# A hybrid decoder step on one core: pools that wait tile by tile, and a 4 MB write moved from the head of the SyncE queue to its tail

## The chip, the core and the metric

The kernel runs on one NeuronCore of a Trainium2 chip. The core has a matrix engine (TensorE, "PE" in the profile, with weight loads "PEld"), a vector engine (DVE), a scalar engine (ACT), GpSimd (POOL) and SyncE (SP), which here only issues transfers. Each engine works through its own instructions in order and waits on semaphores. Transfers are carried by 16 DMA engines; those issued by SP go through one queue (q1, "hardware_dynamic"), those issued by POOL through another (q0, "software_dynamic"). The metric is the device time of one execution in microseconds (us), the median of the runs shown.

## The reference

The program is one inference step of a two-layer decoder: 1024 new prompt tokens with 16 meta tokens ahead of them, and 8 running sequences with one new token each ("the samples"). Layer 0 mixes with gated linear attention, layer 1 with differential attention; each is followed by a squared-ReLU MLP, and every residual goes through a layer norm. All values are 32-bit floats. Cut to what matters:

```python
for layer in range(DEPTH):                       # 2
    if layer % 2 == 0:
        f_p, st_p = gla_prompt(x_p, ...)         # 1024 + 16 tokens, chunked recurrence
        f_s, st_s = gla_sample(x_s, state_gla, ...)   # 8 sequences with a 4 MB state
    else:
        f_p, k_p, v_p = diff_prompt(x_p, ...)    # causal attention, 8 heads, two softmaxes
        f_s, k_s, v_s = diff_sample(x_s, cache_k, cache_v, page_table, ...)  # 4096 past rows in pages
    x_p = post_norm(x_p, f_p, ln_mix_g[layer], ln_mix_b[layer])
    x_s = post_norm(x_s, f_s, ln_mix_g[layer], ln_mix_b[layer])
    x_p = post_norm(x_p, sq_relu_mlp(x_p, mlp_w1[layer], mlp_w2[layer]), ln_mlp_g[layer], ln_mlp_b[layer])
    x_s = post_norm(x_s, sq_relu_mlp(x_s, mlp_w1[layer], mlp_w2[layer]), ln_mlp_g[layer], ln_mlp_b[layer])
y_prompt = x_p[:, N_META:]

def post_norm(x, f, g, b):                       # (z - mean) * rsqrt(var + eps) * g + b
    return layer_norm(DEEPNORM_ALPHA * x + f, g, b)
```

The last line of the last norm adds `ln_mlp_b[1]`, one row of 1024 values, to each of the 1024 rows of `y_prompt`.

## The kernel before

**How products are made.** Most products split each 32-bit operand into a high and a low part of a shorter format and sum three matmuls (`mm3`, lines 185 to 188: L186 high x high, L187, L188 the cross terms). For weights, ACT rounds the loaded tile (`raw` or `rw`) to `whi` and POOL subtracts to get `wlo` (L173, L174; in the last MLP L1386, L1387). The samples' products are plain 32-bit matmuls of narrow operands (L271, L276, L440, L494, L511 in the first stage, L1405 in the last).

**The stages.** (1) Prompt rows are loaded and transposed; the GLA layer runs head by head (q, k, v, decay levels, state updates). Among its matmuls stands the whole chain of the samples through layer 0 and up to layer 1's projections: sample weights come through two 1 MB buffers (`swt`, L214 and L220), the products are L271 and L276, the state of each sequence is loaded (L401), used (L404), updated and written back (L408). (2) Output projection and MLP of layer 0, with the key pages of the samples (L728 reads a page number from the table `ptab` on SP, L730 loads the page) multiplied on DVE and POOL beside it. (3) Projections of layer 1 and the value pages (L802). (4) Causal attention head by head, from L1074 on: a mask tile `cmask` and two tiles `vm` are cleared first, scores go through DVE (L1154) into `as`. (5) Output projection and the MLP of layer 1, written as a seven-product scheme: for each of 4 groups of hidden units seven "up" products, then seven "down" products. `operands` loads and splits what one product needs, while the product before it is half done (`mlp1`: `if t == 2: nxt = operands(...)`). `weight_operand` loads four 256 KB tiles of a weight (L1383) on SP; where a term is a difference of two weights a second load adds onto it from POOL (L1385); in some of the down products (in group 3 in the second and third) it also loads the raw rows of w2 for the samples (L1390, tiles `rw`, five buffers) and calls `beside`, the matmul L1405 into the samples' sums. `chip_operand` reads split activations that an earlier group has kept in DRAM (`XH<-xc`, POOL's queue, L1349).

**The end.** `last` scales each finished row tile and adds it into `y_prompt` in DRAM by an accumulating transfer from POOL (L1305, L1311). So `y_prompt` must hold the norm's offset by then: L1505 writes `ln_mlp_b[1]`, broadcast to 1024 rows, 4 MB from DRAM to DRAM on SP's queue. In the source it stands behind the last up product of group 3 (`if g == 3 and up and i == 7`).

**What sets the order.** A planner with a cost model orders each engine's instructions: what is ready sooner goes sooner, ties go by place in the source. L1505 depends on nothing, and the planner puts it near the head of SP's queue. `tc.issue_after(x)` lets the instructions traced in its block stand behind instruction x on the same engine; it sets the order of issue and adds no wait for x to end.

**Pools.** Tiles live in pools. A pool opened over the bytes of a closed one must wait for the users of these bytes. In the kernel before, the first use of such a pool waits for all the users of the closed pools beneath it. The pools of the stages: `gp` to `s2p` in stage 1, then `kp`, `dp`, `dp2`, `pgp` for the decode, `hp`/`ht`, `rp`/`qt`/`ht`, `a1` to `scp` for attention, and `hp`, `ht`, `rwp` for the last MLP.

Of the kernel before, what the change touches and what calls it, by code (L numbers as in the profile page):

```python
# [18 lines left out]
PSUM = bass.MemoryType.PSUM  # L19
# [3 lines left out]
D = 1024  # L23
T = 1024
# [11 lines left out]
PGB = 8  # L36
HOLD = (6, 8)
HTB = 1
# [72 lines left out]
def hybrid_step(ctx, tc, A, dbg=None, upto=9):  # L111
    nc = tc.nc
    V, S, G, TE = nc.vector, nc.scalar, nc.gpsimd, nc.tensor
    dma = nc.sync.dma_start
# [1 line left out]
    def bc(ap, shape, axis):  # L116
        return ap.unsqueeze(axis).broadcast_to(shape)

    cp = ctx.enter_context(tc.tile_pool(name="cp", bufs=1))
    wsp = ctx.enter_context(tc.tile_pool(name="wsp", bufs=2))  # L120
    wrp = ctx.enter_context(tc.tile_pool(name="wrp", bufs=2))
    mm = ctx.enter_context(tc.tile_pool(name="mm", bufs=3, space=PSUM))
    ax = ctx.enter_context(tc.tile_pool(name="ax", bufs=3, space=PSUM))
    sm = ctx.enter_context(tc.tile_pool(name="sm", bufs=2, space=PSUM))

    def mmt():
        return mm.tile([P, 512], F32, name="mmt")
# [1 line left out]
    def axt():  # L129
        return ax.tile([P, 512], F32, name="axt")  # L130
# [58 lines left out]


    p1 = ExitStack()
    gp = p1.enter_context(tc.tile_pool(name="gp", bufs=1))
    g2 = p1.enter_context(tc.tile_pool(name="g2", bufs=2))
    g8 = p1.enter_context(tc.tile_pool(name="g8", bufs=5))
    swp = p1.enter_context(tc.tile_pool(name="swp", bufs=2))
    spool = p1.enter_context(tc.tile_pool(name="spool", bufs=1))
    s2p = p1.enter_context(tc.tile_pool(name="s2p", bufs=2))

    def t2():
        return g8.tile([P, 512], F32, name="t2")  # L200
# [10 lines left out]
    def sload(src):  # L211

        t = swt()
        dma(t.rearrange("p k n -> p (k n)"), src)  # L214
        return t.rearrange("p k n -> p (k n)")
# [292 lines left out]
    for k in range(NB):  # L508
        t = sload(wd[k * P : (k + 1) * P, 0:2048])
# [48 lines left out]
    for h in range(GH):  # L558
# [3 lines left out]
        for c in range(2):  # L562
            cs = slice(512 * c, 512 * c + 512)
            for i in range(2):
# [3 lines left out]
                t = g2.tile([P, 512], F32, name=("gq", "gk")[i])  # L568
# [20 lines left out]
        for c in range(2):  # L589
# [58 lines left out]
            for i in range(4):  # L648
# [8 lines left out]
                t = 4 * c + i  # L657
# [33 lines left out]
        return dbg(locals())  # L691


    kp = ctx.enter_context(tc.tile_pool(name="kp", bufs=1))
    de = ExitStack()
    dp = de.enter_context(tc.tile_pool(name="dp", bufs=1))
    dp2 = de.enter_context(tc.tile_pool(name="dp2", bufs=2))
    pgp = de.enter_context(tc.tile_pool(name="pgp", bufs=PGB))
    bg_at = [10 ** 7]

    @contextmanager
# [230 lines left out]
    def alpha_row(v, op):  # L932

        for j in range(4):
            hs = slice(256 * j, 256 * j + 256)
            r = ht.tile([P, 256], F32, name="ht")
            dma(r, v[:, hs].broadcast_to([P, 256]))
            for t in (0, 4):
                y = Yt[:, t : t + 4, hs]
                rb = bc(r, [P, 4, 256], 1)  # L940
                if op == ALU.mult:
                    steps_v.append(V.scalar_tensor_tensor(y, y, ALPHA, rb, ALU.mult, ALU.mult).ins)
                else:
                    V.scalar_tensor_tensor(y, rb, ALPHA, y, ALU.mult, ALU.add)
            yield j
# [47 lines left out]


    e = ExitStack()
    hp = e.enter_context(tc.tile_pool(name="hp", bufs=1))
    ht = e.enter_context(tc.tile_pool(name="ht", bufs=HTB))
    HH = hp.tile([P, 4, T], F32R, name="HH")
    HL = hp.tile([P, 4, T], F32R, name="HL")
    for u in range(4):  # L1000
# [8 lines left out]


    e = ExitStack()
    rp = e.enter_context(tc.tile_pool(name="rp", bufs=1))
    qt = e.enter_context(tc.tile_pool(name="qt", bufs=3))
    ht = e.enter_context(tc.tile_pool(name="qht", bufs=2))
# [50 lines left out]

    de.close()
    e = ExitStack()
    a1 = e.enter_context(tc.tile_pool(name="a1", bufs=1))
    a2 = e.enter_context(tc.tile_pool(name="a2", bufs=4))
    a3 = e.enter_context(tc.tile_pool(name="a3", bufs=6))  # L1070
    scp = e.enter_context(tc.tile_pool(name="scp", bufs=5))
    CW = 448
    cm = a1.tile([P, CW], F32, name="cmask")
    V.memset(cm[:, : CW - P], 0.0)  # L1074
# [150 lines left out]


    e = ExitStack()
    hp = e.enter_context(tc.tile_pool(name="hp", bufs=1))
    ht = e.enter_context(tc.tile_pool(name="ht", bufs=HTB))
    rwp = e.enter_context(tc.tile_pool(name="rwp", bufs=5))  # L1230
# [23 lines left out]
    def rawt():  # L1254
        return rwp.tile([P, 512], F32, name="rw")
# [80 lines left out]
            dma(A["y_sample"][:, 0, u * 512 : (u + 1) * 512], sev[NM : NM + NS, :])  # L1336

    count = [0, 0]

    def chip_operand(terms, quarter, n, tmp, kept=None):  # L1340


        buf = XH.t[count[0] % 2].rearrange("p k n -> p (k n)")
        count[0] += 1
        parts = [buf[:, i * 4 * TH : i * 4 * TH + 4 * n] for i in range(2)]
        hi, lo = (x.rearrange("p (k n) -> p k n", n=n) for x in parts)
        if kept and kept[1]:
            for i in range(2):
                nc.gpsimd.dma_start(parts[i], kept[0][:, i])  # L1349
# [12 lines left out]
        if kept:  # L1362
            for i in range(2):
                nc.gpsimd.dma_start(kept[0][:, i], parts[i])
        return hi, lo

    def weight_operand(terms, quarter, side=None, beside=None):

        hi, lo = (wsp.tile([P, 2048], F32R, name=n).rearrange("p (k n) -> p k n", n=512) for n in ("whi", "wlo"))
        run = terms[0] == "run"  # L1370

        def src(q, k):
            w, r0, c0 = quarter(*q)
            return w[r0 + k * P : r0 + (k + 1) * P, c0 : c0 + 512]

        for k in range(4):
            if run or (len(terms) > 1 and terms[-1] != "new"):
                t = RW[:, k, :]
            else:
                count[1] += 1  # L1380
                t = wrp.tile([P, 512], F32, name="raw") if count[1] % 7 in (0, 3) else rawt()
            if not run:
                dma(t, src(terms[0], k))  # L1383
            if len(terms) > 1:
                nc.gpsimd.dma_start(t, src(terms[1], k), accum_op=ALU.add)  # L1385
            S.copy(hi[:, k, :], t)  # L1386
            G.tensor_tensor(lo[:, k, :], t, hi[:, k, :].bitcast(F32), op=ALU.subtract)  # L1387
            for q in side or ():
                t = rawt()
                dma(t, src(q, k))  # L1390
                beside(k, t, *q)
        return hi, lo
# [78 lines left out]
    def mlp1():  # L1471
        seq = []
        for g in range(4):
            seq += [(g, 1, i) for i in (1, 2, 5, 6, 4, 3, 7)]
            seq += [(g, 0, i) for i in ((1, 5, 6, 3, 7, 4, 2) if g < 3 else (1, 5, 6, 7, 4, 3, 2))]
        nxt = operands(*seq[0])
        n = 0
        for at, (g, up, i) in enumerate(seq):
            now = nxt
            if not up and i == 1:  # L1480
                if g == 0:
                    with tc.issue_after(steps_v[-1]):
                        list(alpha_row(A["ln_mix_g"][1:2], ALU.mult))
                    beta = alpha_row(A["ln_mix_b"][1:2], ALU.add)
                else:
                    for _ in range(2):
                        next(beta, None)
            for t in range(4):
                if t == 2 and at + 1 < len(seq):
                    nxt = operands(*seq[at + 1])  # L1490
                if up:
                    for c in range(2):
                        n += 1
                        up_tile(g, i, t, c, *now, axt() if n % 2 else mmt())
                    continue
                n += 1
                down_tile(g, i, t, *now, axt() if n % 2 else mmt())
                if g == 3:
                    for c, u in {7: [(1, 1)], 4: [(1, 0)], 3: [(0, 1)], 2: [(0, 0)]}.get(i, ()):
                        yield 4 * c + t, u  # L1500
            if g == 3 and not up and i == 6:
                samples_out()
            if g == 3 and up and i == 7:
                dma(fg, A["ln_mlp_g"][1:2].broadcast_to([P, D]))
                dma(A["y_prompt"][0], A["ln_mlp_b"][1:2].broadcast_to([T, D]))  # L1505
# [32 lines left out]
```

## Time and profile before

| | |
|---|---|
| median of 3 runs | 2943.17 us (2936.04 to 2952.23) |
| profiled execution | 2949.14 us, its span 2946.3 us |
| granted TensorE clock, mean | 0.977 |
| TensorE busy | 2789.4 us (95%) |
| DMA | 647.48 MB, mean 220 GB/s |
| SP's queue / POOL's queue, share of 16 engines | 53.3% / 16.0% |
| length of the write L1505 | 4096 KB |

A row of the timeline gives start, duration, engine, line, operation, tiles and count; in brackets stands the idle time before it and what ended it. `SPq` rows are issues of transfers by SP, so their duration is that of the issue. A 32-bit sample matmul shows as two records, so that a group of four has x8. A row of waits gives who waited for whom, the total in us, how often, and the longest.

### The profile page before, as it was taken

The page shows a single profiled execution, that of the slowest core. Times are in us where ns is not written, and L with a number is a line of the kernel's source. Part 1 is how long each engine was busy: PE and PEld are TensorE (multiplying, and loading weights), DVE is VectorE, ACT ScalarE, POOL GpSimd, SP SyncE. Part 2 cuts the span into 40 slices and gives each one's busy share as a digit, 9 for nine tenths or more (in the row PEclk, how much of TensorE's full clock was granted, in tenths as well). Part 3 has the DMA queues.
Part 4 walks back from the last instruction along what each step waited for, and adds up shares of the span by engine and source line. Part 5 has one row for each costly group of instructions (what it writes and reads, how often), then busy time and mean ns, then how long its engine had stood idle before and what let it go on. Part 6 is the DMA issues. An engine that isn't in the chain of part 4 may idle for free. (4 is left out here: it accounts for less than half of the span.)

```text
span 2946.3 us, 52168 instructions
## 1 busy us (share of the span) xinstructions
PE 2789.4 (95%) x19668; PEld 2274.8 (77%) x19668; DVE 1858.8 (63%) x2972; ACT 1038.9 (35%) x2072; POOL 1123.3 (38%) x871
## 2 busy tenths in 40 slices
PE   7899989999999999999999998989998999999996
PEld 4666667997777777777898896878888889797875
DVE  2464552546977777777757851778637755738278
ACT  2333433242221221131331111667524635345343
POOL 1231212224433333343233331023235766666665
PEclk9999999999999999999999999899999999999998
DMA  9565761513698988989477999355337878796883
GB/s 261 175 214 202 255 209 36 200 51 116 225 341 295 325 309 317 341 302 324 170 246 245 330 350 342 78 118 116 114 104 203 226 226 235 198 282 158 265 212 72
DMA packets 300203, 647.48 MB, mean 220 GB/s; under 512 B 35168, under 2 KB 150880, under 8 KB 288688
## 3 DMA queue, kind: packets, MB, share of 16 engines
q1 hardware_dynamic: 266976, 530.62, 53.3%
q0 software_dynamic: 32976, 113.55, 16.0%
q8 instruction: 154, 2.52, 0.4%
q14 instruction: 97, 0.79, 0.1%
HBM read 586.56 MB, written 45.11 MB: 214 GB/s over the span
## 5 line engine op out<-in xcount | busy, mean ns | idle before, releaser
L174 POOL TENSOR_TENSOR wlo<-raw,whi 128x512 fp32r<-128x512 f32 x256 | 359.6, 1417 | 748.6 <-ACT whi L173 671.2
L186 PE MATMUL mmt<-whi,XH 128*128 128x256 f32 (+1 forms) x1760 | 526.1, 301 | 4.7 <-DVE qr L1042 2.0
L187 PE MATMUL mmt<-wlo,XH 128*128 128x256 f32 (+1 forms) x1760 | 524.9, 299 | 0.9 <-POOL wlo L174 0.9
L186 PE MATMUL mmt<-XH,whi 128*128 128x512 f32 (+1 forms) x1216 | 438.4, 361 | 9.5 <-DVE HL L183 6.7
L188 PE MATMUL mmt<-XH,wlo 128*128 128x512 f32 (+1 forms) x1216 | 436.7, 360 | 0.0
L188 PE MATMUL mmt<-whi,XL 128*128 128x256 f32 x1536 | 434.1, 284 | 1.8 <-DVE XL L183 1.8
L762 DVE TENSOR_REDUCE sc<-pg 128x16 f32<-128x1024 f32 x256 | 309.6, 1214 | 103.0 <-POOL pg L761 99.7
L173 ACT CAST whi<-raw 128x512 fp32r<-128x512 f32 x256 | 152.9, 619 | 611.1 <-PE mmt L188 188.0
L186 PEld LDWEIGHTS mmt<-whi,XH 128*128 128x128 f32 x1760 | 331.4, 189 | 34.6 <-issue 20.0
L187 PEld LDWEIGHTS mmt<-wlo,XH 128*128 128x128 f32 x1760 | 332.8, 189 | 29.1 <-issue 17.6
L187 PE MATMUL mmt<-XL,whi 128*128 128x512 f32 x768 | 311.2, 405 | 0.0
L761 DVE TENSOR_TENSOR pg<-pg,qb 128x1024 f32<-128x1024 f32 x192 | 261.6, 1368 | 63.6 <-DMA pg<-in_cache_k 44.4
L188 PEld LDWEIGHTS mmt<-whi,XL 128*128 128x128 f32 x1536 | 290.2, 189 | 12.3 <-issue 10.0
L186 PEld LDWEIGHTS mmt<-XH,whi 128*128 128x128 f32 x1216 | 233.0, 192 | 49.6 <-DVE HL L183 8.1
L761 POOL TENSOR_TENSOR pg<-pg,qb 128x1024 f32<-128x1024 f32 x64 | 155.8, 2435 | 302.2 <-DMA pg<-in_cache_k 225.9
L188 PEld LDWEIGHTS mmt<-XH,wlo 128*128 128x128 f32 x1216 | 232.8, 192 | 38.8 <-issue 6.3
L186 PE MATMUL mmt<-whi,HH 128*128 128x512 f32 x512 | 205.3, 401 | 1.4 <-DVE Y L986 1.4
L187 PE MATMUL mmt<-wlo,HH 128*128 128x512 f32 x512 | 204.5, 399 | 0.0
L188 PE MATMUL mmt<-whi,HL 128*128 128x512 f32 x512 | 203.7, 398 | 0.0
L187 PEld LDWEIGHTS mmt<-XL,whi 128*128 128x128 f32 x768 | 147.9, 193 | 43.4 <-issue 11.4
L1387 POOL TENSOR_TENSOR wlo<-RW,whi 128x512 fp32r<-128x512 f32 x96 | 150.1, 1651 | 55.0 <-ACT whi L1386 54.6
L1387 POOL TENSOR_TENSOR wlo<-rw,whi 128x512 fp32r<-128x512 f32 x92 | 142.2, 1626 | 37.8 <-ACT whi L1386 32.7
(431 smaller groups left out, 5713.3 us busy)
## 6 DMA issues: line engine op xcount, KB each, us to landing
pg<-in_cache_k SPq DMA_DIRECT2D x256, 512.0 KB, 6.0
pg<-in_cache_v SPq DMA_DIRECT2D x256, 512.0 KB, 5.8
XH<-xc POOLq DMA_DIRECT2D x42, 1032.0 KB, 8.7
raw<-in_mlp_w SPq DMA_DIRECT2D x164, 256.0 KB, 5.0
rw<-in_mlp_w SPq DMA_DIRECT2D x156, 256.0 KB, 5.1
swt<-in_mlp_w SPq DMA_DIRECT2D x32, 1024.0 KB, 5.2
RW<-in_mlp_w POOLq DMA_DIRECT2D x96, 256.0 KB, 7.2
xc<-XH POOLq DMA_DIRECT2D x14, 1032.0 KB, 6.9
```

The lines of the kernel that those rows point to most:

```text
L173: S.copy(hi[:, c], raw)
L174: G.tensor_tensor(lo[:, c], raw, hi[:, c].bitcast(F32), op=ALU.subtract)
L186: TE.matmul(ps, ah, bh, start=first, stop=False)
L187: TE.matmul(ps, ah, bl, start=False, stop=False)
L188: TE.matmul(ps, al, bh, start=False, stop=last)
L761: eng.tensor_tensor(pg, pg, qb, op=ALU.mult)
L762: return V.tensor_reduce(sc[:, n, :], pg.rearrange("p (h d) -> p h d", d=64), op=ALU.add, axis=AX.X).ins
L1387: G.tensor_tensor(lo[:, k, :], t, hi[:, k, :].bitcast(F32), op=ALU.subtract)
```

## The change

All 28 pools on the chip get `reuse_waits="tile"`: a tile of a pool then waits only for the users of the bytes that it itself covers, where before the pool waited as a whole. And the write of the last norm's offset is traced inside `tc.issue_after(loads[-1])`: it stands on SP behind the last weight load that has been traced by then, the fourth of the first down product of group 3. `loads` is a list that `weight_operand` fills.

```diff
-    cp = ctx.enter_context(tc.tile_pool(name="cp", bufs=1))
+    cp = ctx.enter_context(tc.tile_pool(name="cp", bufs=1, reuse_waits="tile"))
...
     count = [0, 0]
+    loads = []
...
             if not run:
-                dma(t, src(terms[0], k))
+                loads.append(dma(t, src(terms[0], k)).ins)
...
             if g == 3 and up and i == 7:
                 dma(fg, A["ln_mlp_g"][1:2].broadcast_to([P, D]))
-                dma(A["y_prompt"][0], A["ln_mlp_b"][1:2].broadcast_to([T, D]))
+                with tc.issue_after(loads[-1]):
+                    dma(A["y_prompt"][0], A["ln_mlp_b"][1:2].broadcast_to([T, D]))
```

The same argument is added to every other pool. In the order that the planner makes of the changed program, SP's queue begins as before but without the write, and ends with `RW<-in_mlp_w` x4, `rw<-in_mlp_w` x1, the write, and then 16 sample loads (L1390 in the kernel before) mixed with 12 weight loads. On TensorE the order differs from the third sample group (the third set of L271) to the end of stage 1, and then again in the sample matmuls L1405 of group 3: five that stood together stand one by one, with two to six other matmuls between. With the pools' argument alone the order of all engines is that of the kernel before.

More of the change, by code (lines that the diff above doesn't have):

```diff
@@ L191, in hybrid_step @@
     p1 = ExitStack()
[L192 to L197, printed above, removed]
+    gp = p1.enter_context(tc.tile_pool(name="gp", bufs=1, reuse_waits="tile"))
+    g2 = p1.enter_context(tc.tile_pool(name="g2", bufs=2, reuse_waits="tile"))
+    g8 = p1.enter_context(tc.tile_pool(name="g8", bufs=5, reuse_waits="tile"))
+    swp = p1.enter_context(tc.tile_pool(name="swp", bufs=2, reuse_waits="tile"))
+    spool = p1.enter_context(tc.tile_pool(name="spool", bufs=1, reuse_waits="tile"))
+    s2p = p1.enter_context(tc.tile_pool(name="s2p", bufs=2, reuse_waits="tile"))
     def t2():
@@ L995, in hybrid_step @@
     e = ExitStack()
-    hp = e.enter_context(tc.tile_pool(name="hp", bufs=1))
-    ht = e.enter_context(tc.tile_pool(name="ht", bufs=HTB))
+    hp = e.enter_context(tc.tile_pool(name="hp", bufs=1, reuse_waits="tile"))
+    ht = e.enter_context(tc.tile_pool(name="ht", bufs=HTB, reuse_waits="tile"))
     HH = hp.tile([P, 4, T], F32R, name="HH")
@@ L1011, in hybrid_step @@
     e = ExitStack()
-    rp = e.enter_context(tc.tile_pool(name="rp", bufs=1))
-    qt = e.enter_context(tc.tile_pool(name="qt", bufs=3))
-    ht = e.enter_context(tc.tile_pool(name="qht", bufs=2))
+    rp = e.enter_context(tc.tile_pool(name="rp", bufs=1, reuse_waits="tile"))
+    qt = e.enter_context(tc.tile_pool(name="qt", bufs=3, reuse_waits="tile"))
+    ht = e.enter_context(tc.tile_pool(name="qht", bufs=2, reuse_waits="tile"))
     gs = kp.tile([P, 1], F32, name="gs")
@@ L1067, in hybrid_step @@
     e = ExitStack()
[L1068 to L1071, printed above, removed]
+    a1 = e.enter_context(tc.tile_pool(name="a1", bufs=1, reuse_waits="tile"))
+    a2 = e.enter_context(tc.tile_pool(name="a2", bufs=4, reuse_waits="tile"))
+    a3 = e.enter_context(tc.tile_pool(name="a3", bufs=6, reuse_waits="tile"))
+    scp = e.enter_context(tc.tile_pool(name="scp", bufs=5, reuse_waits="tile"))
     CW = 448
@@ L1227, in hybrid_step @@
     e = ExitStack()
-    hp = e.enter_context(tc.tile_pool(name="hp", bufs=1))
-    ht = e.enter_context(tc.tile_pool(name="ht", bufs=HTB))
-    rwp = e.enter_context(tc.tile_pool(name="rwp", bufs=5))
+    hp = e.enter_context(tc.tile_pool(name="hp", bufs=1, reuse_waits="tile"))
+    ht = e.enter_context(tc.tile_pool(name="ht", bufs=HTB, reuse_waits="tile"))
+    rwp = e.enter_context(tc.tile_pool(name="rwp", bufs=5, reuse_waits="tile"))
     for c in range(2):
```

18 lines of the change are left out of this document (9 added, 9 removed).

## The prediction

> **What bounds the kernel now.** I read the page first, then the windows for places where TensorE is not busy, then the waits of TensorE, and last the stretches of the timeline round the two places where the moved transfer stands before and after.
>
> ```profile
> PE 2789.4 (95%) x19668; PEld 2274.8 (77%) x19668; DVE 1858.8 (63%) x2972; ACT 1038.9 (35%) x2072; POOL 1123.3 (38%) x871
> ...
> PE 32%; DMA 6%; DVE 6%; issue 2%; POOL 1%; ACT 1%; SPq 0%; POOLq 0%; DVEq 0%; ACTq 0%
> ```
>
> TensorE works 2789 of 2946 us, so the whole idle time is 157 us, and a change that adds and removes no arithmetic can only move that. The windows that the change touches, and the long middle:
>
> ```profile
> 35.00:55.00 20.00, 13.16 (x57) 8.85 (x55) 0.68 (x1) 0.60 (x1) 0.00 (x0) 0.90 0.99 199
> 55.00:60.00 5.00, 0.66 (x4) 0.20 (x8) 0.00 (x0) 0.00 (x0) 0.00 (x0) 0.50 1.01 391
> 75.00:545.00 470.00, 435.69 (x4263) 325.76 (x4256) 230.59 (x518) 178.10 (x441) 103.07 (x64) 0.97 0.53 176
> ...
> 545.00:2800.00 2255.00, 2175.01 (x14519) 1817.09 (x14518) 1499.19 (x2268) 783.18 (x1499) 926.13 (x726) 0.98 0.73 233
> 2811.00:2836.00 25.00, 25.00 (x187) 23.14 (x187) 20.45 (x29) 17.93 (x38) 13.63 (x11) 1.00 0.67 190
> 2836.00:2870.00 34.00, 34.00 (x127) 19.32 (x123) 25.47 (x25) 14.93 (x28) 23.30 (x20) 1.00 0.87 206
> ```
>
> The columns are stretch, length, busy time of TensorE, its weight loads, DVE, ACT and POOL, granted clock, DMA share, GB/s. The middle, 2255 us, has 80 us idle and keeps its order of instructions. From 35 to 55 us the DMA engines are full (0.99) and yet move only 199 GB/s; then they move 391. At the end, from 2811 to 2870, TensorE has no idle time at all: nothing can be gained there, only lost.
>
> **Part 1: the early write leaves.** The 4 MB write of the last norm's offset into y_prompt (L1505) is the 27th row of SP's queue. This is what follows it:
>
> ```profile
> 32.12 0.67 SPq L1505 DMA_DIRECT2D out_y_prompt<-in_ln_mlp_b  x1
> 32.90 0.57 SPq L214 DMA_DIRECT2D swt<-in_gla_w_in  x1
> ...
> 59.34 1.94 PE L271 MATMUL smt<-swt,sx 128*32 128x512 f32 x8 [11.18 <-DMA swt<-in_gla_w_in]
> 61.21 0.80 PE L187 MATMUL mmt<-XL,whi 128*128 128x512 f32 x1
> ...
> 64.77 0.39 PE L186 MATMUL mmt<-XH,whi 128*128 128x512 f32 x1
> 65.00 0.40 PE L187 MATMUL mmt<-XL,whi 128*128 128x512 f32 x1
> ...
> 65.78 1.07 PE L271 MATMUL smt<-swt,sx 128*32 128x512 f32 x8
> 66.78 0.50 PE L187 MATMUL mmt<-XL,whi 128*128 128x512 f32 x1
> ```
>
> The third load of sample weights (swt, 1 MB) is issued right behind the write and lands only at 59.34, 26.4 us later. 4 MB at 199 GB/s are 21 us, which fills just the slow stretch; then the queue delivers at 391. So the write stands in the queue ahead of the load. TensorE waits 11.18 us for it. After the wait it is slow for a while: the sample group takes 1.87 us until the next starts (against 1.00 at 65.78), and the eight matmuls from 61.21 to 64.77 take 3.56 against 8 x 0.23. That is 0.87 + 1.72 = 2.6 us. Gross, the write costs 13.8 us here.
>
> The Trainium skill (TensorE: Matmul & The Clock Gate, "What's actually happening") says that an idle window of some 3.4 us puts the array to half clock until it has been busy for as long. The granted clock of 0.50 from 55 to 60 and the slow matmuls behind it agree; by its rule a wait below 3.4 us costs only itself.
>
> Not all 13.8 us come back. In the changed program's order TensorE reaches this sample group 56 matmuls earlier, that is at 59.34 - 11.18 - 56 x 0.23 = 35.3 us. The load is still issued at about 32.2 to 32.9, since SP is busy with small loads until then, and one such load takes
>
> ```profile
> swt<-in_gla_w_in SPq DMA_DIRECT2D x12, 1024.0 KB, 5.0
> ```
>
> 5.0 us in the one landing that the trace holds: it lands at about 38. TensorE waits some 3 us. The fourth group stands 14 matmuls and a group (4.2 us) behind, a further 1 MB takes 2.7 us at 391 GB/s, so it doesn't wait. **Term: -13.8 + 3 = -10.8 us**; from -6 (should the load take 8 us, as queued small loads may make it) to -13.8.
>
> **Part 2: the rest of the first stage is laid out anew.** With the write gone, the planner places the whole sample chain up to about 545 us some 10 us earlier among the GLA matmuls (some 600 rows of TensorE's order differ). The instructions are the same in number and shape. TensorE's idle time from 75 to 545 is 470 - 435.7 = 34 us, in short waits:
>
> ```profile
> PE axt L608 <- DVE t L348: 4.5, 3, 2.0
> ...
> PE smt L404 <- DMA Y<-in_state_gla: 4.1, 3, 1.6
> ```
>
> (total, times, longest) for DVE's decay levels and for loads of the state; 34 us is all that the stretch can win. How much other gaps will cost cannot be read from this trace; bounds: -15 (nearly half of the idle time filled) to +15 (as much added). I take 0, since the same chain of DVE steps with the same matmuls to fill it stands in both orders.
>
> **Part 3: the write arrives late.** In the new order of SP it stands behind the last weight load of the first down product of the last group of hidden units, and ahead of the loads of raw w2 for the sample rows (L1390). Before:
>
> ```profile
> 2810.27 0.33 SPq L1383 DMA_DIRECT2D rw<-in_mlp_w  x1
> 2812.45 2.50 SPq L1390 DMA_DIRECT2D rw<-in_mlp_w  x2
> 2815.86 0.33 SPq L1383 DMA_DIRECT2D raw<-in_mlp_w  x1
> ...
> 2835.18 1.92 PE L1405 MATMUL smt<-rw,hs 128*32 128x512 f32 x10
> ...
> q0 software_dynamic: 796, 2.60, 39.8%
> q1 hardware_dynamic: 1152, 2.10, 26.2%
> ...
> rw<-in_mlp_w SPq DMA_DIRECT2D x5, 256.0 KB, 7.5
> ```
>
> (the last three rows: queues and sample loads from 2811 to 2836). So it goes out at about 2810.6. Behind it wait 16 sample loads and 12 later weight loads, all on SP's queue. The first consumer is the sample matmul that TensorE reaches at 2835.2. In the early place a load behind the write landed 59.34 - 32.12 = 27.2 us after the write's issue, of which 2 us because it was four times as big: 25.2. So the first sample load lands at 2810.6 + 25.2 = 2835.8 if nothing else is on the engines: lower bound of the stall 0 to 1 us. But POOL's queue (q0) takes 39.8% of these 25 us, 10 us of engine time, which the early place did not have. Added in full, the load lands at 2845.8, and TensorE waits 10.6 us, with 2.6 us of slow clock behind as at 61 us: upper bound 13. Since the early write left no idle engine time (0.99), I put the value near the upper end: **+9 us**. TensorE has no gap up to 2870, so the delay goes through to the end, where DVE follows it. Later sample loads come in five buffers, and the new order spaces their matmuls 1.2 to 2.3 us apart; a quarter-MB load takes 0.7 us at 391 GB/s, so I count nothing for them. The additions into y_prompt come long after:
>
> ```profile
> L1305 POOL DMA_DIRECT2D out_y_prompt<-Y x6: 865/884/963, 2914.4 to 2931.4; - x6
> ```
>
> at 2914, 70 us behind the write. Their wait costs nothing.
>
> On sharing, the Trainium skill (DMA: Bandwidth & Descriptors, "Queues, rings and completion order") says that each DMA engine takes turns between the queues that have work, a packet at a time. By that rule q0's 10 us come out of the write's time in full, the term is +13 and the sum +2 in place of -2; no run here shows a 4 MB write beside q0.
>
> **Part 4: pools wait tile by tile.** This leaves the order of every engine as it was; only some 35 waits name other semaphores. The one stage border where a pool's wait shows is the start of attention:
>
> ```profile
> POOL vm L1082 <- SPq L728: 47.1, 1, 47.1
> DVE cmask L1074 <- SPq L728: 11.2, 1, 11.2
> ...
> PE axt L1111 <- DVE XL L183: 6.8, 1, 6.8
> ...
> 1837.08 0.23 DVE L818 COPY oT<-smt 128x4 f32<-128x4 f32 x2 [6.15 <-PE smt L816]
> 1837.63 0.52 DVE L1154 CUSTOM_DVE_ANT_0 as<-mmt,cmask 128x352 f32<-128x352 f32 x1 [0.32 <-DMA wlo<-out_k_rows_p]
> ```
>
> TensorE's 6.8 us come from DVE, which is held by the mask's memset until SP has read the page table for the last time (L728). In the changed program this memset still waits for SP: the mask lies on those bytes. POOL's memset (vm) is freed, but nothing of TensorE's waits for it. The first score tile no longer waits for ACT and POOL, but it is queued on DVE behind the copy at 1837.08, which ends the decode in both. **Term: 0**, from -3 (the memset of vm and POOL's moves behind it come early) to +1.
>
> **Sum.** -10.8 + 0 + 9 + 0 = -1.8 us. The profiled execution took 2949.1 us (span 2946.3); it is 6.0 above the median of 2943.2, to which I apply the difference: 2941.4, say **2941**. A measurement of this kernel can tell about 0.5% (14.7 us; the three runs lie 16 us apart).
>
> **Rivals.**
> - *The late write is hidden.* Its engine time fits: from 2811 to 2836 the share is 0.67, so 8 us are free, and the first sample load, landing at 2812.5 + 7.5 = 2820, has 15 us of lead. Against: 21 us don't fit into 8. Late term 0 to 2: 2943.2 - 10.8 + 1 = 2933.
> - *Turns between the queues starve both.* Then POOL's loads of the last up product's operand suffer too:
>
> ```profile
> 2806.89 1.13 POOL L1349 DMA_DIRECT2D XH<-xc  x2
> ...
> 2829.17 0.28 PE L186 MATMUL mmt<-XH,whi 128*128 128x258 f32 x1
> 2829.29 0.28 PE L187 MATMUL mmt<-XH,whi 128*128 128x258 f32 x1
> ...
> XH<-xc POOLq DMA_DIRECT2D x42, 1032.0 KB, 8.7
> ```
>
> They land at about 2816, and TensorE needs them at 2818 (the product is 8 tiles of 12 matmuls, 0.12 us apart, and ends with these rows). Two waits, each with slow clock: 13 + 2.6 - 10.8 = +5: 2948.
> - *The new layout of the first stage decides*, by another -15 to +15 (part 2).
> - *Slower: the write is not what held the load.* If the 4-byte rows of the small loads ahead clog the queue, swt still lands near 59. Then TensorE, which now comes at 35.3, waits 24 us rather than 11: 12.9 worse, +9 at the end: 2965. It decides once the load lands after 48. Against: the switch from 199 to 391 GB/s just as 4 MB are through.
>
> **How the numbers follow.** Forecast 0.42 (2941, give or take 9); hidden write 0.17 (2933); starved queues 0.18 (2948); layout 0.15 (2928 to 2958); write innocent 0.08 (2965). Faster by over 0.5% (below 2928.5): 0.03 + 0.07 + 0.05 = 0.15. Slower (above 2957.9): 0.03 + 0.05 + 0.06 + 0.07 = 0.21. Within: 0.64. The range runs from 2927, the hidden write with some gain in layout, to 2960, which leaves out the last rival. The likeliest case's own range is 2932 to 2950.
>
> **What would show it.** Right: no wait above 5 us of L271 for swt near 38 us, and no stretch at 199 GB/s from 35 to 55; TensorE 10 us ahead near 100 us; a wait of L1405 for rw of 5 to 11 us near 2830; the same 6.8 us at the start of attention. Wrong: no wait at L1405, or waits at the last up product; idle time from 75 to 545 that is not 34 +- 10; a cmask memset that starts early.

## The result and the profile after

The changed kernel takes 2928.17 us (median of 20 runs, 2919.04 to 2941.66), the kernel before 2940.66 us (20 runs, 2930.12 to 2953.5). The ratio is 0.9961, 95% interval 0.9949 to 0.9974: about 11.5 us less, which is within the 0.5% below which the prediction counted no change. The profiled execution took 2936.23 us (span 2934.5, mean clock 0.980) against 2949.14 us: 12.9 us less.

Where the time went is read by comparing when TensorE starts the same instruction in both traces. Against the kernel before, the changed kernel is 26.3 us early when stage 1 ends, still 26.4 us early at 2790 us, and 12.8 us early at 2870 us. So more came in early, and more was given back late, than the sum of the prediction had. These offsets come from one profile of each kernel, and the profile of the kernel before is of an execution 8.5 us longer than its median of 2940.66, so they are good to a few us only; the experiments say how few.

The early place. The first fence is the timeline of the changed kernel, the second its windows (length, busy time of TensorE, weight loads, DVE, ACT, POOL, then clock, DMA share, GB/s), the third the three largest waits of TensorE from 75 us to the end of stage 1 at 518.7 us (total, times, longest).

```profile
32.52 0.38 SPq L214 DMA_DIRECT2D swt<-in_gla_w_in  x1
32.99 0.38 SPq L171 DMA_DIRECT2D raw<-in_gla_w_in  x1
33.47 0.42 SPq L214 DMA_DIRECT2D swt<-in_gla_w_in  x1
...
39.46 1.94 PE L271 MATMUL smt<-swt,sx 128*32 128x512 f32 x8 [4.23 <-DMA swt<-in_gla_w_in]
41.32 0.61 PE L187 MATMUL mmt<-XL,ghi 128*16 128x512 f32 x1
...
44.72 0.51 PE L186 MATMUL mmt<-XH,ghi 128*16 128x512 f32 x1
```

```profile
35.00:55.00 20.00, 15.77 (x65) 8.13 (x65) 1.96 (x3) 3.56 (x6) 5.15 (x4) 0.83 0.96 349
75.00:518.70 443.70, 421.89 (x4201) 320.16 (x4202) 234.78 (x517) 179.86 (x439) 105.20 (x62) 0.99 0.52 175
...
2814.00:2820.00 6.00, 6.00 (x9) 1.84 (x9) 2.45 (x2) 0.34 (x1) 4.43 (x5) 0.50 1.07 304
```

```profile
PE smt L404 <- DMA Y<-in_state_gla: 3.8, 2, 3.3
PE mmt L186 <- ACT Y L586: 3.1, 2, 2.7
PE axt L608 <- DVE t L348: 3.0, 5, 1.7
```

The stretch at 199 GB/s is gone (349 now). The wait for the third sample load fell from 11.18 to 4.23 us. TensorE is still slow behind it: the sample group takes 1.86 us until the next start instead of 1.00, and the eight matmuls from 41.32 to 44.72 take 3.40 instead of 8 x 0.23. That is 2.4 us, so the place costs 6.6 where it cost 13.8: 7.2 us won. The other 19.1 us come from the rest of stage 1. Its idle time fell from 34.3 (470 - 435.69) to 21.8 us (443.7 - 421.89), 12.5 us; the rest, some 6.5 us, is TensorE's clock, 0.99 where it was 0.97. That short waits alone can bring the slow clock shows in two windows of the kernel before:

```profile
136.00:143.00 7.00, 3.39 (x148) 2.36 (x140) 6.90 (x19) 1.56 (x4) 0.00 (x0) 1.00 0.35 86
143.00:150.00 7.00, 5.97 (x16) 4.88 (x17) 2.83 (x7) 1.34 (x3) 2.88 (x2) 0.52 0.97 312
```

In the first, TensorE works half of the time, and no single wait from 130 to 150 us is longer than 1.7 us; in the second, its clock is 0.52.

The late place, in the timeline of the changed kernel:

```profile
2784.27 0.65 SPq L1507 DMA_DIRECT2D out_y_prompt<-in_ln_mlp_b  x1
2786.06 4.04 SPq L1391 DMA_DIRECT2D rw<-in_mlp_w  x2
...
2813.98 1.92 PE L1406 MATMUL smt<-rw,hs 128*32 128x512 f32 x2 [4.63 <-DMA rw<-in_mlp_w]
2815.83 0.80 PE L188 MATMUL axt<-whi,XH 128*128 128x512 f32 x1
...
2818.26 1.89 PE L1406 MATMUL smt<-rw,hs 128*32 128x512 f32 x2
2820.08 0.50 PE L187 MATMUL axt<-wlo,XH 128*128 128x512 f32 x1
...
2821.43 1.04 PE L1406 MATMUL smt<-rw,hs 128*32 128x512 f32 x2
2822.41 0.50 PE L186 MATMUL mmt<-whi,XH 128*128 128x512 f32 x1
```

The first sample load lands 29.7 us after the write's issue (2813.98 - 2784.27). TensorE waits 4.63 us and then runs at a clock of 0.50 from 2814 to 2820, which costs 2.8 us (two sample groups 0.9 each, five matmuls 1.1 in all). A third part was in none of the prediction's terms: the sample matmuls. Alone, one takes 0.98 us (2821.43 to 2822.41). In the kernel before, five together (x10) took 1.85 us in all, up to the next start:

```profile
2835.18 1.92 PE L1405 MATMUL smt<-rw,hs 128*32 128x512 f32 x10
2837.03 0.50 PE L186 MATMUL axt<-whi,XH 128*128 128x512 f32 x1
```

The changed order has 14 single ones and one pair, the order before a five, a four and seven singles. A group of four takes 1.85 us as well, and a pair 1.83, so what counts is how many separate groups there are. At these prices the order before comes to 10.6 us and the changed one to 15.6 at full clock. The step into a group and the step out of it cost 0.1 us each (there a start follows the one before by 0.33 us, between large matmuls by 0.23), and there are 15 groups in place of nine: another 1.2 us. Together that is some 6 us. The three parts are weighed by runs below.

The pools, in the waits of the changed kernel from 1790 to 1850 us:

```profile
DVE cmask L1074 <- SPq L728: 12.3, 1, 12.3
...
PE axt L1111 <- DVE XL L183: 7.6, 1, 7.6
```

Both waits at the start of attention are there as before (11.2 and 6.8). GpSimd's wait of 47.1 us for the same reading of the page table is gone, as the prediction said of `vm`, and TensorE gained nothing by it.

### The profile page after: what moved, and what is told of

The parts are those of the page before. It is cut to its first block, busy times and chain, and to the rows that moved or that the text cites. A ratio compares the mean times of both kernels' runs of the same rounds, so it can differ in the third digit from the quotient of the medians.

```text
span 2934.5 us, 52166 instructions
## 1 busy us (share of the span) xinstructions
PE 2788.3 (95%) x19668; PEld 2269.2 (77%) x19668; DVE 1856.4 (63%) x2972; ACT 1044.0 (36%) x2075; POOL 1131.2 (39%) x871
## 4 chain that ended last, share of the span: by engine, by line
PE 73%; DVE 10%; DMA 10%; issue 3%; POOL 2%; ACT 2%; SPq 1%; POOLq 0%; DVEq 0%; ACTq 0%
PE mmt L186 17%; PE mmt L187 17%; PE mmt L188 17%; PE smt L802 4%; PE axt L186 2%; PE axt L188 2%; PE axt L187 2%; PE smt L1174 2%; DMA rw<-in_mlp_w 2%; DMA XH<-xc 1%; PE smt L440 1%; PE smt L1406 1%; DVE pg L761 1%; PE axt L1169 1%; DMA RW<-in_mlp_w 1%
## 5 line engine op out<-in xcount | busy, mean ns | idle before, releaser
L187 PEld LDWEIGHTS mmt<-wlo,XH 128*128 128x128 f32 x1760 | 332.6, 189 | 24.7 <-issue 13.8
```

Source lines behind the costliest of these rows:

```text
L187: TE.matmul(ps, ah, bl, start=False, stop=False)
```

## The experiments

All ratios are to the kernel before, run on the same chip beside them. "Offset" is again how much earlier or later than in the kernel before TensorE starts the same instruction. The edits are shown against the changed kernel in runs 1 to 8 and 12, and against the kernel before in runs 9 to 11. One caution on size: single profiles of one order differ. The change and run 2 have the same order on every engine and are 9.6 us of offset apart at 2790 us. Run 1, with the order of the kernel before, shows an offset of -2.8 at the end of stage 1 and of -12.1 at 2790. Eight profiles have the changed kernel's order of TensorE in stage 1 (the change, runs 2 to 7 and 12), and their stages end with offsets from -22.9 to -30.0, 26 in the mean. So single profiles are read by stages and not by their ends, and a difference of less than some 7 us at the end of stage 1 says nothing.

**1. The pools alone.** The argument `reuse_waits="tile"` on all pools, the write as before:

```diff
-                with tc.issue_after(loads[-1]):
-                    dma(A["y_prompt"][0], A["ln_mlp_b"][1:2].broadcast_to([T, D]))
+                dma(A["y_prompt"][0], A["ln_mlp_b"][1:2].broadcast_to([T, D]))
```

> The pools' new rule alone; the write of the offset stays early, and every engine's order is that of the kernel before. Theory (the write's move does it all): ratio 1.000, from 0.998 to 1.001 (0 us, -3 to +1 as in the prediction). TensorE still waits 11 us for the third load of sample weights near 59 us and 7 us at the start of attention. Rival (the tile by tile waits carry a good part of the 11.5 us): 0.996 to 0.998, with idle time gone at the borders of the stages.

Measured: 2942.91 us, ratio 0.9996 (0.9978 to 1.0014). Two of TensorE's waits in this run, from 35 to 75 us and at the start of attention:

```profile
PE smt L271 <- DMA swt<-in_gla_w_in: 10.6, 1, 10.6
...
PE axt L1111 <- DVE XL L183: 7.5, 1, 7.5
```

The pools do nothing that can be measured.

**2. The write's move alone.** The argument of the pools is taken back on all of them, one of which is shown.

```diff
-    cp = ctx.enter_context(tc.tile_pool(name="cp", bufs=1, reuse_waits="tile"))
+    cp = ctx.enter_context(tc.tile_pool(name="cp", bufs=1))
...
```

> The write's move alone, pools as before; order of every engine as in the changed kernel. Theory: ratio 0.996 (0.995 to 0.9975), the same as the changed kernel. Rival (pools carry a part): 0.998 to 1.000. A second rival (the pools' rule is what makes the late part dear or cheap): differs from the changed kernel by more than 0.2%.

Measured: 2928.08 us, ratio 0.9943 (0.9926 to 0.9960); its interval overlaps that of the change. The offset is -25.5 us at the end of stage 1, and in the tail it loses 14.3 (-36.0 at 2790, -21.7 at 2870). Both effects of the change belong to the write.

**3. No write.** What the write costs in all in its late place; `y_prompt` then lacks the norm's offset.

```diff
-                with tc.issue_after(loads[-1]):
-                    dma(A["y_prompt"][0], A["ln_mlp_b"][1:2].broadcast_to([T, D]))
```

> The changed kernel without the 4 MB write at all (y_prompt then lacks the last norm's offset). Stage 1 has the order of the changed kernel, the tail has the sample matmuls in groups again, as the kernel before has. Theory (early side gains 26 us, the late place gives 13.7 back): ratio 0.991, 26 us under before and 13 to 14 under the changed kernel; no wait of the first sample matmul for its load. Rival 1 (the late write is hidden, the tail loses the time to something else): equal to the changed kernel, 0.996. Rival 2 (the gain of stage 1 is one profile's chance): 0.995 to 0.998, with TensorE's idle time from 75 us to the end of stage 1 at 30 us or more.

Measured: 2915.38 us, ratio 0.9901 (0.9881 to 0.9921). Offset -24.3 at the end of stage 1, -24.9 at 2790, -24.2 at 2870. The early gain stands, and the tail loses nothing; so the late loss is the write's. The two rivals fall.

**4. Half the write, late.** The other half of `y_prompt` lacks the offset.

```diff
-                    dma(A["y_prompt"][0], A["ln_mlp_b"][1:2].broadcast_to([T, D]))
+                    dma(A["y_prompt"][0, 512:], A["ln_mlp_b"][1:2].broadcast_to([512, D]))
```

> The changed kernel with a late write of half the rows (512 of 1024; the other half of y_prompt lacks the offset), in the same place of SP's queue. The sample matmuls come in groups again. It tells the wait from the grouping. Theory: half the write is 10.5 us of the engines' time in place of 21; the first sample load lands 10 us earlier and is there when TensorE comes, so no wait, no slow clock, no single matmuls: 0.991, within 1.5 us of the kernel without the write. Rival (the queue holds the load for a fixed time, or the turns between the queues do it, whatever the size): a wait of 4 to 5 us stays, and as the matmuls come earlier than in the changed kernel it is 5 to 8 us; ratio 0.994.

Measured: 2922.2 us, ratio 0.9917 (0.9897 to 0.9936); offset -24.3 at 2790 and -23.7 at 2870, no wait of L1406. Half the size costs nothing in the tail: the loads behind it have enough lead for 2 MB, not for 4.

**5. The late write in eight pieces, earlier in the last stage.**

```diff
                     nxt = operands(*seq[at + 1])
+                    if 14 <= at < 30 and at % 2 == 0:
+                        r = slice((at - 14) * 64, (at - 14) * 64 + P)
+                        with tc.issue_after(loads[-1]):
+                            dma(A["y_prompt"][0, r], A["ln_mlp_b"][1:2].broadcast_to([P, D]))
...
-                with tc.issue_after(loads[-1]):
-                    dma(A["y_prompt"][0], A["ln_mlp_b"][1:2].broadcast_to([T, D]))
```

> The changed kernel, with the late write cut into 8 writes of 128 rows (0.5 MB each), each queued behind a weight load of the second and third group of hidden units, some 600 to 400 us before the end, where TensorE needs the next operand only a product later. The sample matmuls of the tail come in groups as before. Theory (the late price is the 21 us of engine time at one place of the queue): each piece delays what stands behind it by 2.6 us, which those loads have as lead; no wait in the tail. Ratio 0.991 (0.989 to 0.993), as without any write: a version that beats both. Rival (TensorE has no gap there and the loads have no lead: engine time is paid wherever it falls): 8 x 2.6 us come back somewhere, 0.994 to 0.998, with waits on operands between 2150 and 2550 us.

Measured: 2920.23 us, ratio 0.9934 (0.9908 to 0.9959), just outside the theory's own range and inside the gap to the rival's. The pieces went out from 2347 to 2540 us. The offset is -27.5 both at 2790 and at 2870, so the tail is free. Between 2130 and 2500 us it stays at -32; the 4.5 us up to 2790 are lost behind the pieces and are within the drift between profiles.

**6. The late write on ScalarE's queue.**

```diff
-                with tc.issue_after(loads[-1]):
-                    dma(A["y_prompt"][0], A["ln_mlp_b"][1:2].broadcast_to([T, D]))
+                with tc.issue_after(acts[-1]):
+                    nc.scalar.dma_start(A["y_prompt"][0], A["ln_mlp_b"][1:2].broadcast_to([T, D]))
```

(`acts` collects the casts of the weights on ScalarE, as `loads` collects the loads.)

> The late write issued from ScalarE's queue rather than SP's, at about the same time (behind the last weight cast); the sample matmuls are spaced singly as in the changed kernel. It tells the place in the queue from the share of the engines. Theory (the loads of SP's queue stand behind the write because they share a queue): the first sample load shares the engines with the write by turns and lands within some 15 us of its issue, before TensorE comes; the wait of 4.6 us and the slow clock (2.7) go, the single matmuls' 5 us stay: 7 us under the changed kernel, ratio 0.9935. Rival (the engines are full, whoever issues): the wait stays at 4 us or more, 0.996. Second rival (turns starve the other queue too): waits also at the last up product's operands, over 0.996.

Measured: 2924.86 us, ratio 0.9942 (0.9922 to 0.9963). The timeline, and the queues from 2785 to 2815 us:

```profile
2784.24 2.50 SPq L1392 DMA_DIRECT2D rw<-in_mlp_w  x2
...
2790.62 0.65 ACTq L1508 DMA_DIRECT2D out_y_prompt<-in_ln_mlp_b  x1
2793.77 2.57 SPq L1392 DMA_DIRECT2D rw<-in_mlp_w  x2
...
2807.01 1.90 PE L1407 MATMUL smt<-rw,hs 128*32 128x512 f32 x4
2811.84 1.04 PE L1407 MATMUL smt<-rw,hs 128*32 128x512 f32 x2
2813.48 1.04 PE L1407 MATMUL smt<-rw,hs 128*32 128x512 f32 x2
...
2819.39 1.02 PE L1407 MATMUL smt<-rw,hs 128*32 128x512 f32 x2 [0.94 <-DMA rw<-in_mlp_w]
```

```profile
q10 hardware_dynamic: 1010, 4.10, 49.9%
q0 software_dynamic: 695, 1.72, 26.5%
q1 hardware_dynamic: 1201, 2.20, 26.2%
```

The first two sample loads left 6 us ahead of the write, so they tell nothing. The third and fourth left at 2793.8, 3 us behind it, and if the loads are used in their order, they were there at 2811.84 and 2813.48, less than 20 us later; behind the write in one queue a load took 27.9 us (2786.06 to 2813.98). The engines were as full (share 1.03). So place in the queue counts: ScalarE's queue (q10) took 49.9% of the engines' time, and SP's (q1) moved its 2.2 MB beside it. The packets show it more directly: from 2798 to 2812 us the write's queue moved 572 and SP's queue 506, nearly one for one, while in the changed kernel, from 2798 to 2810, SP's queue with the write at its head had 99.4% of the engines' time. The wait of 4.63 and the slow clock became one wait of 0.94: against the change this run gains 6.7 us of offset in the tail. Against run 3 (groups, no write) it loses 6.9 there. Less the 0.9 of its wait, 6.0 us remain, and the sample matmuls, two pairs and twelve single ones here, are what the two orders of the tail differ in. The prices per group from above give 5.9 us for these 14 groups against the nine of run 3.

**7. The late write one step later,** behind the loads of the next product (the edit of run 5, with `if seq[at] == (3, 0, 6)` in place of the condition and the whole write).

> The late write moved one place on, behind the sample loads and weight loads of the next products, so that the first sample load is ahead of it; the sample matmuls come in groups. Theory: the first sample matmul finds its load (no wait there), but the five-buffer ring of later sample loads and the weight loads of the next product stand behind the write's 21 us; TensorE reaches those some 25 us later, so the wait is 0 to 5 us, and without single matmuls the ratio is 0.992 to 0.994. Rival (any place of the tail costs the same, since the engines' 21 us come out of a tail that has no gap): 0.996, with the wait of 5 us or more at a later load.

Measured: 2926.18 us, ratio 0.9951 (0.9934 to 0.9969), dearer than expected though the intervals touch. The write leaves at 2829.8. No sample load is late, but the weights behind it are: of TensorE's waits from 2800 to 2900

```profile
PE axt L186 <- DVE Y L1459: 2.0, 1, 2.0
...
PE mmt L187 <- POOL wlo L1388: 0.9, 1, 0.9
PE axt L187 <- POOL wlo L1388: 0.8, 1, 0.8
PE mmt L186 <- ACT whi L1387: 0.7, 1, 0.7
```

the last three are splits of late weights. Against run 3 it loses 3.4 us of offset from 2840 to 2925 us.

**8. The whole write in the middle of stage 1,** behind the last write-back of a state, with yet another order of stage 1.

```diff
-        dma(A["gla_state_s"][0, b].rearrange("h d e -> d h e"), stt)
+        wb = dma(A["gla_state_s"][0, b].rearrange("h d e -> d h e"), stt).ins
+    with tc.issue_after(wb):
+        dma(A["y_prompt"][0], A["ln_mlp_b"][1:2].broadcast_to([T, D]))
```

> The write whole, behind the last write-back of a state in stage 1 (about 160 us); stage 1 is laid out in yet another order, the tail as in the kernel before. It samples what the layout alone does. Theory (the order of the sample chain in stage 1 is worth up to 15 us, and the write costs only what waits behind it): the tail loses nothing; stage 1 ends between 11 and 26 us earlier than in the kernel before, less up to 11 us for loads behind the write; ratio 0.991 to 0.998. Rival (layout is worth nothing, the 26 us of stage 1 are the write's own): a write inside stage 1 costs about the same as the early one, 0.998 to 1.001.

Measured: 2938.36 us, ratio 0.9984 (0.9968 to 1.0000); offset -2.2 at the end of stage 1. The first wait was as short as in the change (4.1), and the write at 152.7 us made another:

```profile
PE smt L442 <- DMA swt<-in_gla_w_out: 10.9, 1, 10.9
PE axt L610 <- DVE gAd L619: 4.7, 1, 4.7
```

This went as the rival said: a write in stage 1 seemed to cost its 22 to 26 us wherever it stood. The next two runs put that to the test with smaller writes.

**9. An early write of 64 rows.** The other rows of `y_prompt` lack the offset.

```diff
-                dma(A["y_prompt"][0], A["ln_mlp_b"][1:2].broadcast_to([T, D]))
+                dma(A["y_prompt"][0, 960:], A["ln_mlp_b"][1:2].broadcast_to([64, D]))
```

> The kernel before with an early write of only 64 rows (0.25 MB) in the old place; the other rows of y_prompt lack the offset. The planner lays out stage 1 in an order of its own, unlike that of before and of the changed kernel; the tail is that of before. Theory now (a whole write costs stage 1 some 22 to 26 us of its own wherever it stands there, through the sample chain that it delays; the order has little to do with it): stage 1 ends 23 to 27 us before that of the kernel before, ratio 0.991 (0.990 to 0.993). Rival (15 of the 26 us are the luck of one order): with another order, and the direct 11 us gone, the end comes anywhere from 0 to 26 us early, ratio 0.993 to 0.998.

Measured: 2930.21 us, ratio 0.9972 (0.9958 to 0.9987); offset only -11.6 at the end of stage 1. The theory taken over from run 8 falls. The third load, the window from 75 us on, and the largest waits there:

```profile
39.82 1.06 PE L271 MATMUL smt<-swt,sx 128*32 128x512 f32 x8 [4.08 <-DMA swt<-in_gla_w_in]
```

```profile
75.00:533.40 458.40, 425.80 (x4179) 324.07 (x4178) 230.61 (x516) 180.63 (x440) 103.36 (x62) 0.97 0.51 170
```

```profile
PE axt L608 <- DVE t L348: 7.4, 4, 2.3
PE smt L494 <- DMA swt<-in_mlp_w: 4.5, 3, 2.6
PE smt L404 <- DMA Y<-in_state_gla: 4.2, 4, 1.8
```

The direct gain is there (a wait of 4.1 in place of 11.2; the eight matmuls from 41.06 to 44.47 us behind it still take 3.41 instead of 8 x 0.23), and nothing else: idle time of 32.6 us and a clock of 0.97, as in the kernel before (34.3, 0.97). Run 3, with no write and the changed kernel's order, ends stage 1 12.7 us earlier. A write of 0.25 MB, 1.3 us by the rate of 199 GB/s, does not account for that. Nor is it one profile's chance: over all executions the two ratios, 0.9972 and 0.9901, have intervals that lie apart. What is left is the order.

**10. An early write of 512 rows** (the same edit with 512).

> The kernel before with an early write of half the rows (2 MB, 10.5 us of engine time at 199 GB/s), again in an order of its own; the other half of y_prompt lacks the offset. Theory (price by size): the third sample load lands some 10 us earlier, at about 49, TensorE still waits for it, since it comes earlier too (3 to 13 us); stage 1 ends 10 to 16 us before that of before: ratio 0.9955 (0.994 to 0.997). Rival 1 (the order decides, not the size): more than 4 us away from half of the whole write's price. Rival 2 (the small loads ahead hold the queue, not the write): 0.999 or more, with the stretch at about 200 GB/s as long as before.

Measured: 2925.59 us, ratio 0.9951 (0.9934 to 0.9967): the ratio that the theory gave, for another reason. The stage ends with an offset of -21.6, where half of the whole write's price would be some 13: the first rival held. That is ten us before run 9, though the write is eight times as big and the third load later:

```profile
47.47 1.93 PE L271 MATMUL smt<-swt,sx 128*32 128x512 f32 x8 [5.71 <-DMA swt<-in_gla_w_in]
```

The landing does go by size: 59.34 us behind 4 MB, 47.47 behind 2, 39.82 behind 0.25, and TensorE waits for it in each. The end of the stage does not. The ten us between runs 9 and 10 rest on one profile of each; the ratios of the two, 0.9972 and 0.9951, still overlap.

| run | write in stage 1 | third load used at | its wait | idle after 75 us | offset at the end |
|---|---|---|---|---|---|
| before | 4 MB early | 59.34 | 11.2 | 34.3 | 0 |
| 9 | 0.25 MB early | 39.82 | 4.1 | 32.6 | -11.6 |
| 10 | 2 MB early | 47.47 | 5.7 | 25.0 | -21.6 |
| 3 | none | 39.63 | 4.6 | 21.3 | -24.3 |
| change | none | 39.46 | 4.2 | 21.8 | -26.3 |

**11. The early write, whole, on ScalarE's queue.**

```diff
-                dma(A["y_prompt"][0], A["ln_mlp_b"][1:2].broadcast_to([T, D]))
+                nc.scalar.dma_start(A["y_prompt"][0], A["ln_mlp_b"][1:2].broadcast_to([T, D]))
```

> The kernel before with the early write, whole, issued from ScalarE's queue; SP's queue holds loads alone. Theory (what counts is who stands behind the write in its queue): the sample loads share the engines by turns and come 10 us or more earlier than behind it; the wait for the third sample load falls from 11 to under 6 us; ratio 0.993 to 0.996. Rival (the engines are full for 21 us whoever issues, and every load shifts by as much): the stage ends as before, 0.999 to 1.001.

Measured: 2944.26 us, ratio 1.0013 (0.9996 to 1.0030). This did not test what it was made for. With nothing ahead of it on that queue the write left at 0.79 us, and took its turns from the loads of the prompt. TensorE's waits up to 75 us:

```profile
PE axt L255 <- DMA Y<-in_x_prompt: 19.6, 6, 10.8
...
PE smt L271 <- DMA swt<-in_gla_w_in: 0.5, 1, 0.5
```

The wait moved from the samples to the prompt, and the stage ended as before (+1.0). Another queue helps only where the loads beside it have lead.

**12. The write in two halves,** one in the place of the change, one 340 us ahead of it.

```diff
                     nxt = operands(*seq[at + 1])
+                    if at == 20:
+                        with tc.issue_after(loads[-1]):
+                            dma(A["y_prompt"][0, :512], A["ln_mlp_b"][1:2].broadcast_to([512, D]))
...
                 with tc.issue_after(loads[-1]):
-                    dma(A["y_prompt"][0], A["ln_mlp_b"][1:2].broadcast_to([T, D]))
+                    dma(A["y_prompt"][0, 512:], A["ln_mlp_b"][1:2].broadcast_to([512, D]))
```

> The changed kernel with the late write in two halves: rows 512 to 1023 in the place of the change, rows 0 to 511 behind a weight load of the second group of hidden units; TensorE keeps the order of the kernel without the write, sample matmuls in groups. Theory (a half is free at each of the two places): no wait of a sample matmul for its load, no loss from 2790 us on, ratio 0.9915 (0.990 to 0.9935), a complete kernel that beats the changed one by 0.2 to 0.6%. Rival (the engine time has to be paid wherever it falls): one of the two halves brings a wait of 5 us or more, 0.994 to 0.996.

Measured: 2918.25 us, ratio 0.9932 (0.9908 to 0.9956). The halves leave at 2438.5 and 2779.6. From 2790 to 2846 TensorE has no idle time and the full clock, and the five sample matmuls stand together again:

```profile
2790.00:2846.00 56.00, 56.00 (x262) 38.30 (x261) 42.52 (x49) 29.61 (x56) 35.15 (x28) 1.00 0.82 205
```

```profile
2804.17 1.92 PE L1406 MATMUL smt<-rw,hs 128*32 128x512 f32 x10
```

This complete kernel is faster than the one before. By the medians it is some 10 us below the changed one too; the two intervals (0.9908 to 0.9956, 0.9949 to 0.9974) still touch, so that is likely and not settled.

## Why the prediction was right or wrong

The time of 2928.2 lies in the range, 1.2 us above its lower end, and by its ratio in the class that got 0.64; as a time it is just below the 2928.5 named there, but the kernel before measured 2940.7 beside it and not 2943.2. The likeliest value, 2941, was 13 us too high, and the time is below that case's own range of 2932 to 2950. As a difference, -1.8 us was forecast and about -11.5 measured. That it is no farther off is partly luck: one term came out 19 us cheaper than forecast and two others 3.6 and 4.7 us dearer. The rival "the new layout of the first stage decides" came about, with 0.15. (Its 2928 to 2958 sets the 15 us about 2943; about the forecast of 2941 they give 2926 to 2956.)

- **The early write leaves: -10.8 predicted, -7.2 measured.** What held the load was the write, as argued: the load follows the write's size (runs 9 and 10). TensorE came at 35.2, as worked out (35.3). The load landed at 39.5 and not at 38, so the wait was 4.2 and not 3, and the slow clock that the prediction left out came behind it, 2.4 us. The rule of the Trainium skill (TensorE: Matmul & The Clock Gate, "What's actually happening"), by which idle time of some 3.4 us halves the clock, agrees where waits are long: 4.23 us of wait, and the slow matmuls behind it. What the prediction took from the rule, that a wait below 3.4 us costs only itself, does not agree with the trace: in the kernel before the clock is 0.52 from 143 to 150 us, behind several waits of at most 1.7 us.
- **The rest of the first stage: 0 predicted, -19 measured, good to a few us. This is the step that failed.** "I take 0, since the same chain of DVE steps with the same matmuls to fill it stands in both orders" was wrong, and the bound of -15 was too narrow too: it counted idle time alone, and the order also moved the clock, worth some 6.5 us. The prediction's own sign of being wrong, idle time outside 34 +- 10, came about with 21.8. Runs 3 and 9 show that the order moves the end of the stage by more than 10 us with hardly any write, and runs 9 and 10 against the write's size. What in the changed order does it isn't settled: every move of the write gives another order, and no run could hold the order and vary the write in stage 1.
- **The late write: +9 predicted, 13.7 measured, above the upper bound of 13.** The landing was right (25.2 to 35.2 us behind the issue predicted, 29.7 measured), the wait of 4.6 just under the 5 to 11 named, and the slow clock of 2.8 us is that of the upper bound. The missing term is the new spacing of the sample matmuls, 6 us (run 6 against run 3, and the prices per group), for which the prediction counted nothing though it named the spacing. The rival of a hidden write falls with run 3.
- **Queues.** By the rule of taking turns (the Trainium skill, DMA: Bandwidth & Descriptors, "Queues, rings and completion order") the prediction had the term at +13. Run 6 agrees with the rule: a write on its own queue left room for SP's loads, 506 packets beside its 572. Within one queue no turn showed: the load behind was used 27.9 us after its issue in the changed kernel, and the later the larger the write ahead (runs 9 and 10).
- **Pools: 0 predicted, 0.9996 measured.** Right, with the waits at the start of attention where they were. The starved product of the rival "turns between the queues" did not show: the change's only wait of TensorE from 2790 to 2870 is that of L1406.

## What to carry to other kernels

A bulk transfer that nothing needs soon is not free: it delays what stands behind it in its queue, and this costs time where the loads behind have less lead than the transfer takes. Cut it until each piece is shorter than the lead of the loads behind it, and put the pieces where there is lead; half of this one cost nothing in a place where the whole cost 14 us. And when moving it lets a planner lay out a long stage anew, give that layout a wide range of its own, clock included: here it was larger than the direct term.

## What the runs showed of the hardware

- A 4 MB broadcast from DRAM to DRAM holds what is behind it in its queue, and the longer the larger it is: the load was used at 59.3, 47.5 and 39.8 us behind 4, 2 and 0.25 MB (39.5 and 39.6 behind none), 19.5 us for 3.75 MB, about the 199 GB/s of the stretch.
- Narrow 32-bit sample matmuls into different parts of one sum are much cheaper when four or five stand together: four or five in 1.85 us, one alone in 0.98 us. A pair, at 1.83 us, saved next to nothing. Spacing them out to wait less for each load cost as much as the wait.
- An order of instructions can cost or save several us by the clock alone: from 75 us to the end of stage 1 the mean clock was 0.97 in the kernel before, in run 1 and in run 9, and 0.98 or 0.99 in the eight profiles with the changed order. It is not only long waits that do it: 143 to 150 us in the kernel before ran at 0.52 behind waits of at most 1.7 us.
